# Four projections of a two-layer decoder trunk as seven half-products instead of eight, on one Trainium2 core

## The chip, the cores and the metric

The kernel runs on one core of a Trainium2 chip. TensorE (PE) multiplies matrices into PSUM, VectorE (DVE), ScalarE (ACT) and GpSimd (POOL) work on tiles, and the queue of SyncE (SP) issues the loads. The metric is device time in microseconds. The kernel before takes 1397.26 us, the median of 3 runs from 1395.95 to 1399.61.

## The reference

Input x is 512 tokens by 1024 features, c one conditioning vector. Two layers follow each other, then a final RMSNorm. Everything is fp32. One layer, cut to what matters:

```
h = rmsnorm(x, norm_w) * (1 + scale) + shift          # scale, shift, gate: from c @ w_ada
qa, ka, va, za, qr, kr, vr, zr, ga, gr = split(h @ w_in)   # 1536 x3, 512, 1024 x6 columns
y_att = dilated_attention(qa, ka, va) * silu(za)      # 512 x 512, three window patterns, joined by softmax
y_ret = groupnorm(retention(rot(qr), rot(kr), vr)) * silu(zr)   # 512 x 1024, four heads of 256
merged = sigmoid(ga) * (y_att @ w_proj_attn) + sigmoid(gr) * (y_ret @ w_proj_ret)
x = x + gate * (merged @ w_out)
```

The change concerns the products for ga, gr, y_ret @ w_proj_ret and merged @ w_out. Each is 512 x 1024 by 1024 x 1024.

## The kernel before

Every fp32 factor is split into a high part (a rounded copy) and a low part (the rest): `split` (L151) lets ScalarE cast the source to `hi` and VectorE subtract `hi` from the source to get `lo`. A product is then three matmuls, hi by hi, hi by lo and lo by hi (`mm3`, L175), accumulated in PSUM. Weights come from DRAM in tiles `wst` of 512 KB (128 partitions x 2 x 512 or 4 x 256 elements), issued on SyncE's queue (`weights`, L162), and are split into `wh` and `wl`.

The core does one thing after another for a layer: projections and attention for two pairs of head slots, then four retention heads (`ret_q`, `ret_k`, `ret_z`, `ret_scores`, `ret_v`, `ret_out`, `ret_y`), then gates, merge and output (`layer`, L754). Up to the merge the activations are feature-major: features on partitions, 512 tokens along a row, with the weights as the stationary side. `gate` (L700) makes 256 features of a gate at a time; `merge` (L708) multiplies the attention projection (4 blocks of 128 inputs) and the retention projection (8 blocks) by their gates and splits the sum; its result is the stationary side of `out_block` (L741), which makes one block of 128 tokens by 512 columns, token-major, from w_out held in SBUF (`out_weights`, L729). Blocks 0 to 3 of the second half of the columns end one after the other, and each that is complete calls `on_block`: at the end of layer 0 `next_layer` (L829), which normalizes the block and turns it for layer 1, at the end of layer 1 `result` (L843), which scales and stores it. x lives in four SBUF tiles `xb`, updated in place.

A tile scheduler orders each engine's instructions ahead of time, after the program's order and its own model of when what is ready. Tiles come from pools of a fixed count of slots for each tag (`NB`, L70); a tile whose slot is still in use waits. Work for the conditioning vector (`ada`, L197: a vector-matrix product on VectorE) and the gate rows is a `background` list, of which `step` (L157) does a piece at each weight load. All loads go through one queue, in the order in which they are issued.

## Time and profile before

| | us | share of the span |
|---|---|---|
| profiled execution | 1397.1 | |
| its span | 1395.3 | |
| TensorE busy | 1354.1 | 97% |
| VectorE busy | 833.5 | 60% |
| ScalarE busy | 487.7 | 35% |
| GpSimd busy | 161.3 | 12% |

TensorE is busy nearly from end to end; its granted clock over the span is 0.994 of full. The DMA engines move 106 GB/s on average, 148.06 MB in all. A row of the profile gives line, engine, operation, output and inputs; the time of one is its mean, and the idle time named with it is that of the engine just before it, with what ended it.

### The profile page before, as it was taken

The numbers are of one execution on the slowest core, as the hardware profiler recorded it, in microseconds if no ns is written. First come the engines' busy times: TensorE is split into PE (matmuls) and PEld (weight loads), VectorE is DVE, ScalarE is ACT, GpSimd is POOL, SyncE is SP. The second block draws the span as 40 slices with busy tenths as digits, with TensorE's granted clock in tenths as the row PEclk, the third lists the DMA queues.
The fourth block names the chain that finished last, engine by engine and source line by source line (L and its number), as shares of the span: only waits on it lengthen the run. The fifth ranks groups of instructions, "written<-read, shape, count | busy, mean of one in ns | idle before, by whom it ended". The sixth has DMA issues, their size and how long they took to land.

```text
span 1395.3 us, 17913 instructions
## 1 busy us (share of the span) xinstructions
PE 1354.1 (97%) x7033; PEld 1177.4 (84%) x7033; DVE 833.5 (60%) x1492; ACT 487.7 (35%) x863; POOL 161.3 (12%) x140
## 2 busy tenths in 40 slices
PE   3899999999999999999999999999999999999997
PEld 3778978888888888888888898888898898888886
DVE  6887678786547554335656646556745656533444
ACT  4352433253233243224333325234432233422322
POOL 3500000031102121000030001002111211100001
PEclk9899999999999999999999999999999999999999
DMA  9746145322222232224613232122232222222511
GB/s 309 229 151 181 61 137 166 112 71 84 79 96 91 69 98 91 91 91 159 201 49 106 76 91 90 61 91 76 76 92 75 91 89 71 91 91 91 169 42 61
DMA packets 136404, 148.06 MB, mean 106 GB/s; under 512 B 5056, under 2 KB 125056, under 8 KB 136320
## 3 DMA queue, kind: packets, MB, share of 16 engines
q1 hardware_dynamic: 136320, 146.92, 33.3%
q8 instruction: 55, 0.90, 0.3%
q14 instruction: 29, 0.24, 0.0%
HBM read 144.81 MB, written 2.10 MB: 105 GB/s over the span
## 4 chain that ended last, share of the span: by engine, by line
PE 90%; DVE 5%; DMA 1%; SPq 1%; issue 1%; ACT 1%; POOL 0%; POOLq 0%; DVEq 0%; ACTq 0%
PE ps_mm L180 80%; PE ps_aux L180 5%; PE ps_po L186 1%; DVE f L536 1%; SPq L194 1%; DVE acc L208 1%; PE ps_aux L565 1%; DVE wl L153 1%; PE ps_aux L186 1%; DMA pt<-in_w_ada 1%; PE ps_po L187 1%; PE ps_aux L679 1%; DMA v<-in_w_ada 0%; POOL h L294 0%; DVE qk L153 0%
## 5 line engine op out<-in xcount | busy, mean ns | idle before, releaser
L180 PE MATMUL ps_mm<-h,wh 128*128 128x512 f32 x2176 | 681.0, 393 | 5.1 <-DVE qk L153 2.1
L180 PEld LDWEIGHTS ps_mm<-h,wh 128*128 128x128 f32 x2176 | 406.7, 189 | 87.4 <-DVE qk L153 2.3
L180 PE MATMUL ps_mm<-h,wl 128*128 128x512 f32 x1088 | 424.6, 393 | 3.9 <-DVE wl L153 3.6
L153 DVE TENSOR_TENSOR wl<-wst,wh 128x1024 fp32r<-128x1024 f32 x194 | 244.7, 1264 | 227.7 <-ACT wh L152 225.4
L152 ACT CAST wh<-wst 128x1024 fp32r<-128x1024 f32 (+1 forms) x202 | 210.3, 1045 | 349.4 <-PE ps_mm L180 275.6
L180 PEld LDWEIGHTS ps_mm<-h,wl 128*128 128x128 f32 x1088 | 204.9, 189 | 46.1 <-DVE wl L153 4.5
L180 PE MATMUL ps_mm<-wh,h 128*128 128x256 f32 (+1 forms) x960 | 213.5, 316 | 0.2 <-POOL h L294 0.2
L180 PEld LDWEIGHTS ps_mm<-wh,h 128*128 128x128 f32 x960 | 180.8, 223 | 1.4 <-POOL h L294 0.6
L180 PE MATMUL ps_mm<-wl,h 128*128 128x256 f32 (+1 forms) x480 | 150.4, 315 | 0.0
L180 PEld LDWEIGHTS ps_mm<-wl,h 128*128 128x128 f32 x480 | 106.9, 223 | 0.2
L618 POOL TENSOR_TENSOR tmp<-tmp,tmp 128x512 f32<-128x512 f32 x32 | 49.2, 1554 | 458.6 <-ACT wh L152 234.1
L153 DVE TENSOR_TENSOR v<-ps_mm,v 128x256 fp32r<-128x256 f32 (+1 forms) x52 | 24.0, 463 | 61.7 <-ACT v L152 61.6
L152 ACT CAST qk<-ps_mm 128x512 fp32r<-128x512 f32 x48 | 27.8, 586 | 94.0 <-PE ps_mm L180 94.0
L208 DVE SCALAR_TENSOR_TENSOR acc<-pt,sc,acc 128x256 f32<-128x256 f32 x112 | 58.9, 526 | 2.6
L180 PE MATMUL ps_mm<-v,wh 128*128 128x512 f32 x192 | 59.1, 389 | 0.0
L152 ACT CAST v<-ps_mm 128x256 fp32r<-128x256 f32 (+1 forms) x52 | 20.9, 406 | 97.4 <-PE ps_mm L180 97.4
L180 PE MATMUL ps_aux<-qk,qk 128*128 128x256 f32 (+3 forms) x288 | 47.8, 307 | 0.0
L180 PEld LDWEIGHTS ps_aux<-qk,qk 128*128 128x128 f32 x288 | 42.9, 190 | 3.4
L153 DVE TENSOR_TENSOR qk<-ps_mm,qk 128x512 fp32r<-128x512 f32 x48 | 32.8, 686 | 19.6 <-ACT qk L152 19.6
L180 PEld LDWEIGHTS ps_mm<-v,wh 128*128 128x128 f32 x192 | 36.0, 188 | 7.5
L704 ACT ACTIVATE y<-ps_mm 128x512 f32<-128x512 f32 x32 | 19.0, 594 | 58.8 <-PE ps_mm L180 58.8
L180 PE MATMUL ps_mm<-s,wh 128*128 128x512 f32 x128 | 39.4, 389 | 0.0
(196 smaller groups left out, 1569.1 us busy)
## 6 DMA issues: line engine op xcount, KB each, us to landing
wst<-in_w_in SPq DMA_DIRECT2D x170, 512.0 KB, 3.6
pt<-in_w_ada SPq DMA_DIRECT2D x36, 512.0 KB, 5.0
wst<-in_w_proj_ret SPq DMA_DIRECT2D x16, 512.0 KB, 3.4
wst<-in_w_out SPq DMA_DIRECT2D x16, 512.0 KB, 3.6
qk<-in_w_ada SPq DMA_DIRECT2D x8, 512.0 KB, 8.6
wst<-in_w_proj_attn SPq DMA_DIRECT2D x8, 512.0 KB, 3.4
wst<-in_w_in SPq DMA_DIRECT2D x8, 384.0 KB, 6.6
v<-in_w_ada SPq DMA_DIRECT2D x8, 256.0 KB, 5.2
```

The lines of the kernel that those rows point to most:

```text
L152: nc.scalar.copy(hi, src)
L153: (nc.gpsimd if pool else nc.vector).tensor_tensor(lo, src, f(hi), op=ALU.subtract)
L180: nc.tensor.matmul(ps_ap, a, b_, start=first and i == 0, stop=last and i == n - 1, skip_group_check=skip)
L186: nc.tensor.matmul(ps_ap, st[0], mv, start=first, stop=False, skip_group_check=skip)
L187: nc.tensor.matmul(ps_ap[:, 0:P], st[1], mv[:, 0], start=False, stop=last, skip_group_check=skip)
L194: nc.sync.dma_start(s_, src[:, i:i + per])
L208: nc.vector.scalar_tensor_tensor(acc, w_, c_, acc, op0=ALU.mult, op1=ALU.add)
L536: nc.vector.tensor_copy(f0[32 * cc:32 * cc + 32, b], f0c[32 * b:32 * b + 32, cc])
L565: nc.tensor.transpose(blk(ps, j), src, ident)
L618: nc.gpsimd.tensor_tensor(a, a, b_, op=ALU.subtract if i == 0 else ALU.add)
L679: nc.tensor.transpose(ps[:, (2 * i + j) * P:(2 * i + j + 1) * P], self.rn[2 * b2 + j][:, i * P:(i + 1) * P], ident)
L704: nc.scalar.activation(s_, ps, AF.Sigmoid)
```

## The change

Each of the four products is cut in half along tokens, inner dimension and columns, into 2 x 2 blocks: A11 to A22 for the activations (256 tokens by 512 inputs), W11 to W22 for the weights (512 x 512). Eight products of blocks would be the plain way. `pair` does seven, with sums of blocks on either side: with S1 = A21 - A22, S2 = S1 - A11, S4 = S2 + A12 and S3 = A11 - A21, the products are A11 by W11, A12 by W21, S1 by (W11 + W12), S4 by W22, S2 by (W11 + W12 + W22), S3 by (W22 + W12) and A22 by (W11 + W12 + W22 + W21). They are done in the order 11, 12, S1, S4, S2, S3, 22, each as 24 matmuls of 512 columns with a token block as the stationary side, so the results are token-major. Outputs come from sums of products: block (0,0) after product 12, (0,1) after S2, (1,1) after S3, (1,0) after 22.

The weight sums are made while loading: `add` is a DMA on GpSimd's queue that adds the source in DRAM to a tile already in SBUF. One pair of tiles ("x") holds W11 and takes W12, W22 and W21 in turn, each after the split of the sum before; another ("z") holds W22 and takes W12; W21 is loaded plainly. The activation sums are made by `combined`: on GpSimd for h (used for both gates), on VectorE for retention's output (`combine_y`) and for the merged inputs (`combine_m`). `merge_att` makes the attention projection token-major, merges, and turns the merged blocks by TensorE. The multiplications by za move to the end of the last retention head. x is not kept in SBUF: it is loaded again at the output projection (`result`), from `x1d`, a DRAM tensor written by `next_layer`, in layer 1. The pools change: h, s, v and y have half as many slots of twice the size, and wst seven slots instead of three.

The core of the diff:

```
-    NB = dict(h=16, qk=6, s=8, v=12, pt=4, y=12, tmp=4, wst=3, wh=4, wl=4, dec=1)
+    NB = dict(h=8, qk=6, s=4, v=6, pt=4, y=6, tmp=4, wst=7, wh=4, wl=4, dec=1)
...
-    xb = [big.tile([P, D], F32, tag=f"x{b}", name=f"x{b}", bufs=1) for b in range(4)]
+    xs = [T("s", F32, (P, D)) for b in range(4)]
+    dram = ctx.enter_context(tc.tile_pool(name="dram", bufs=1, space=bass.MemoryType.DRAM))
+    x1d = dram.tile([S, D], F32, name="x1d")
...
+        def pair(self, src, rows0, nk, j0, A, buf, done):
+            step()
+            n = nk // 2
+            def part(r, c, i):
+                r0, c0 = rows0 + (r * n + 2 * i) * P, j0 + c * S
+                return src[r0:r0 + 2 * P, c0:c0 + S].rearrange("(k p) j -> p k j", p=P)
+            def load(r, c):
+                ts = [T("wst", F32, (P, 2, S)) for _ in range(n // 2)]
+                for i, t in enumerate(ts):
+                    nc.sync.dma_start(t, part(r, c, i))
+                return ts
+            def add(ts, r, c):
+                for i, t in enumerate(ts):
+                    nc.gpsimd.dma_start(t, part(r, c, i), accum_op=ALU.add)
+                return ts
+            def parts(ts):
+                res = []
+                for t in ts:
+                    hi, lo = T2("wh"), T2("wl")
+                    split(t, hi, lo)
+                    res.append((hi, lo))
+                return res
+            chain = {}
+            def weights_of(i):
+                if i == 0:
+                    chain["x"] = load(0, 0)
+                    return parts(chain["x"])
+                if i == 1:
+                    return parts(load(1, 0))
+                if i == 3:
+                    chain["z"] = load(1, 1)
+                    return parts(chain["z"])
+                return parts(add(chain["z"], 0, 1) if i == 5 else
+                             add(chain["x"], *{2: (0, 1), 4: (1, 1), 6: (1, 0)}[i]))
+            def product(a, w, ps, first):
+                for u in range(2):
+                    mm3(ps[u], [(A[a](k, u), (w[k // 2][0][:, k % 2], w[k // 2][1][:, k % 2])) for k in range(n)],
+                        first=first, skip=True)
+            b, c, e = [PS(), PS()], None, None
+            x1, x5 = {}, {}
+            names = ["11", "12", "S1", "S4", "S2", "S3", "22"]
+            ws = [weights_of(0)]
+            for i, a in enumerate(names):
+                if i + 1 < len(names):
+                    ws.append(weights_of(i + 1))
+                w = ws[i]
+                if i == 0:
+                    product(a, w, b, True)
+                    for u in range(2):
+                        x1[u] = buf(0, 0, u)
+                        nc.scalar.copy(x1[u], b[u])
+                elif i == 1:
+                    e = [PS("po"), PS("po")]
+                    product(a, w, e, True)
+                    for u in range(2):
+                        nc.vector.tensor_tensor(x1[u], e[u], x1[u], op=ALU.add)
+                        done(0, 0, u, x1[u])
+                elif i == 2:
+                    c = [PS(), PS()]
+                    product(a, w, c, True)
+                    for u in range(2):
+                        x5[u] = buf(1, 1, u)
+                        nc.scalar.copy(x5[u], c[u])
+                elif i == 3:
+                    product(a, w, c, False)
+                elif i == 4:
+                    product(a, w, b, False)
+                    for u in range(2):
+                        t = buf(0, 1, u)
+                        nc.scalar.copy(t, b[u])
+                        nc.vector.tensor_tensor(t, c[u], t, op=ALU.subtract)
+                        done(0, 1, u, t)
+                elif i == 5:
+                    product(a, w, b, False)
+                    for u in range(2):
+                        nc.vector.tensor_tensor(x5[u], x5[u], b[u], op=ALU.subtract)
+                        done(1, 1, u, x5[u])
                 else:
+                    product(a, w, b, False)
+                    for u in range(2):
+                        done(1, 0, u, b[u])
+        def combined(self, terms, n, tags, eng, own=True):
...
+            for name in ("S1", "S4", "S2", "S3"):
+                tile_(name)
+            for i in range(n // 2):
+                t = T("tmp").rearrange("p (k t) -> p k t", k=2)
+                a11, a12, a21, a22 = (terms(r, c, i) for r in range(2) for c in range(2))
+                def less(o, a, b):
+                    eng.tensor_tensor(o, a[0], b[0], op=ALU.subtract)
+                    if len(a) == 2:
+                        t2 = T("tmp").rearrange("p (k t) -> p k t", k=2)
+                        eng.tensor_tensor(t2, a[1], b[1], op=ALU.subtract)
+                        eng.tensor_tensor(o, o, t2, op=ALU.add)
+                less(t, a21, a22)
+                put("S1", i, t)
+                for a in a11:
+                    eng.tensor_tensor(t, t, a, op=ALU.subtract)
+                put("S2", i, t)
+                for a in a12:
+                    eng.tensor_tensor(t, t, a, op=ALU.add)
+                put("S4", i, t)
+                t3 = T("tmp").rearrange("p (k t) -> p k t", k=2)
+                less(t3, a11, a21)
+                put("S3", i, t3)
...
+        def gates(self, off, tag):
+            g = [T(tag, F32, (P, 2, S)) for _ in range(4)]
+            at = lambda r, c, u: g[2 * r + u][:, c]
+            self.pair(self.win, 0, KT, off, self.A, at,
+                      lambda r, c, u, ap: nc.scalar.activation(at(r, c, u), ap, AF.Sigmoid))
+            return g
+        def combine_y(self):
...
+            self.A = self.combined(terms, 4, ["s", "s", "v", "v", "h", "h", "h", "h", "qk", "qk", "qk", "qk", "qk", "qk"],
+                                   nc.vector)
+        def merge_ret(self):
+            def done(r, c, u, ap):
+                g = self.gr[2 * r + u][:, c]
+                nc.vector.tensor_tensor(g, ap, g, op=ALU.mult)
+            self.pair(w_proj_ret[self.l], 0, KT, 0, self.A, lambda r, c, u: T("tmp"), done)
+        def merge_att(self):
...
+            self.mT = [[T("y", F32, (P, 4, CW)) for c in range(2)] for r in range(2)]
+            for b in range(4):
+                for c in range(2):
+                    ps, g = PS(), self.ga[b][:, c]
+                    mm3(ps, [((blk(ya[k][0], b), blk(ya[k][1], b)), tuple(t[:, k % 2] for t in wa[2 * c + k // 2]))
+                             for k in range(4)])
+                    nc.vector.tensor_tensor(g, ps, g, op=ALU.mult)
+                    nc.vector.tensor_tensor(g, g, self.gr[b][:, c], op=ALU.add)
+                    ps = PS("aux")
+                    for k in range(4):
+                        nc.tensor.transpose(blk(ps, k), blk(g, k), ident)
+                    o = self.mT[b // 2][c][:, :, (b % 2) * P:(b % 2 + 1) * P]
+                    nc.scalar.copy(o, ps.rearrange("p (k t) -> p k t", k=4))
+        def combine_m(self):
...
+            self.A = self.combined(terms, 4, ["h"] * 8 + ["qk"] * 6, nc.vector)
+        def result(self, xin, on_block):
+            xt = []
+            for b in range(4):
+                xt.append(T("pt", F32, (P, D)))
+                nc.sync.dma_start(xt[b], xin[b * P:(b + 1) * P])
+            ssq = [small([P, 2], "ssq", 4) for b in range(4)]
+            left = [2] * 4
+            def done(r, c, u, ap):
+                b = 2 * r + u
+                cols = slice(c * S, (c + 1) * S)
+                t = T("tmp")
+                nc.vector.tensor_tensor(t, ap, gate_bc[self.l][:, cols], op=ALU.mult)
+                nc.vector.tensor_tensor(xt[b][:, cols], xt[b][:, cols], t, op=ALU.add)
+                nc.scalar.activation(t, xt[b][:, cols], AF.Square, accum_out=ssq[b][:, c:c + 1])
+                left[b] -= 1
+                if not left[b]:
+                    on_block(b, xt[b], rms(b, ssq[b]))
+            self.pair(w_out[self.l], 0, KT, 0, self.A, lambda r, c, u: T("tmp"), done)
...
-        L.ys, L.mg = [], []
-        L.split_y(0, 4)
-        ga = [L.gate(GA, 0)]
+        L.combine_h()
+        L.za(0)
         L.ret_out(RETH - 1)
-        gr = [L.gate(GR, 0)]
+        L.za(1)
+        L.ga = L.gates(GA, "v")
         L.ret_y(RETH - 1)
-        L.split_y(4, 12)
-        for m in range(1, 4):
-            ga.append(L.gate(GA, m))
-            gr.append(L.gate(GR, m))
-            L.merge(m - 1, ga[m - 1], gr[m - 1])
-        w0 = L.out_weights(0, ["h"] * 16)
-        L.merge(3, ga[3], gr[3])
-        ssq = [small([P, 3], "ssq", 4) for b in range(4)]
-        w1 = L.out_weights(1, ["v"] * 12 + ["s"] * 4)
-        for b in range(4):
-            L.out_block(0, b, w0, ssq)
-        for b in range(4):
-            L.out_block(1, b, w1, ssq)
-            on_block(b, rms(b, ssq[b][:, 0:3 if b == 3 else 2]))
+        L.gr = L.gates(GR, "pt")
+        L.combine_y()
+        L.merge_ret()
+        L.merge_att()
+        L.combine_m()
+        L.result(xin, on_block)
...
-    def next_layer(b, r):
-        xn.append(normalize(b, r))
+    def next_layer(b, x_, r):
+        nc.sync.dma_start(x1d[b * P:(b + 1) * P], x_)
+        xn.append(normalize(x_, r))
...
-    layer(L0, next_layer)
+    layer(L0, x, next_layer)
...
-    layer(L1[0], result)
+    layer(L1[0], x1d, result)
```

Three places show what moves. The first is VectorE at the output projection of layer 0. Before, it has there the gate and residual operations of the blocks (L750, L751; x_69 to x_72 are the four blocks of x) and the background's modulation (L208):

```order
L750 TENSOR_TENSOR tmp_5827<-ps_mm_5826,gate_89 128x512
L208 SCALAR_TENSOR_TENSOR acc_6248<-pt_6255,sc,acc_6248 128x256
L751 TENSOR_TENSOR x_69<-x_69,tmp_5827 128x512
L208 SCALAR_TENSOR_TENSOR acc_6248<-pt_6255,sc,acc_6248 128x256
L750 TENSOR_TENSOR tmp_5856<-ps_mm_5855,gate_89 128x512
L208 SCALAR_TENSOR_TENSOR acc_6248<-pt_6255,sc,acc_6248 128x256
L751 TENSOR_TENSOR x_70<-x_70,tmp_5856 128x512
```

After, from the last sums for S1 to the first operands of S4, between the products S1 and S2. Here y_5659 to y_5662 are the merged inputs, tmp_5851 and tmp_5865 the running sums (L838, L841 are `combined`), qk_5848, qk_5850, qk_5880 and h_5846 the low parts for S2, S3, 22 and S4, ps_po the sums of product 12 (L776), and wl_6042 the low part of the first weight tile for S2:

```order
L838 TENSOR_TENSOR tmp_5851<-tmp_5851,y_5659 128x512
L838 TENSOR_TENSOR tmp_5865<-tmp_5865,y_5659 128x512
L155 TENSOR_TENSOR qk_5848<-tmp_5851,qk_5847 128x512
L155 TENSOR_TENSOR qk_5848<-tmp_5865,qk_5847 128x512
L841 TENSOR_TENSOR tmp_5851<-tmp_5851,y_5660 128x512
L155 TENSOR_TENSOR qk_5850<-tmp_5861,qk_5849 128x512
L841 TENSOR_TENSOR tmp_5865<-tmp_5865,y_5660 128x512
L155 TENSOR_TENSOR qk_5850<-tmp_5875,qk_5849 128x512
L155 TENSOR_TENSOR qk_5880<-y_5662,qk_5879 128x512 x2
L155 TENSOR_TENSOR h_5846<-tmp_5851,h_5845 128x512
L776 TENSOR_TENSOR tmp_5947<-ps_po_5961,tmp_5947 128x512
L155 TENSOR_TENSOR wl_6042<-wst_5899,wh_6041 128x1024
```

The sums and splits of the merged inputs now stand on VectorE ahead of wl_6042.

The second place is VectorE at the boundary from layer 0 to layer 1. Before, at the end of the last token block (x_72; L293 modulates a turned block of layer 1, L282 normalizes, L146 is part of the root mean square):

```order
L750 TENSOR_TENSOR tmp_6102<-ps_mm_6101,gate_89 128x256
L750 TENSOR_TENSOR tmp_6131<-ps_mm_6130,gate_89 128x256
L751 TENSOR_TENSOR x_72<-x_72,tmp_6102 128x256
L751 TENSOR_TENSOR x_72<-x_72,tmp_6131 128x256
L293 TENSOR_SCALAR tmp_6174<-ps_aux_6169,mod_a_86,mod_s_88 128x256
L273 TENSOR_REDUCE ssum_6159<-ssq_5785 128x1
L146 TENSOR_SCALAR rn_t_6161<-ssum_6159 128x1
L293 TENSOR_SCALAR tmp_6178<-ps_aux_6169,mod_a_86,mod_s_88 128x256
L282 TENSOR_SCALAR y_6165<-x_72,rn_6163 128x512
L282 TENSOR_SCALAR y_6166<-x_72,rn_6163 128x512
```

After, from the first half of product 22 on (ps_mm_5897; pt_5889, pt_5891 and pt_5887 are blocks 2, 3 and 1 of x, L936 and L937 the gate and the residual addition, L285 normalizes, L296 modulates, L208 and L210 are the background, wl_6512 and wl_6518 weights of layer 1):

```order
L936 TENSOR_TENSOR tmp_6209<-ps_mm_5897,gate_92 128x512
L937 TENSOR_TENSOR pt_5891<-pt_5891,tmp_6181 128x512
L285 TENSOR_SCALAR y_6138<-pt_5887,rn_6135 128x512 x2
L208 TENSOR_SCALAR acc_6350<-pt_6351,sc 128x256
L937 TENSOR_TENSOR pt_5889<-pt_5889,tmp_6209 128x512
L155 TENSOR_TENSOR wl_6512<-wst_6509,wh_6511 128x1024
L210 SCALAR_TENSOR_TENSOR acc_6350<-pt_6351,sc,acc_6350 128x256
L155 TENSOR_TENSOR wl_6518<-wst_6515,wh_6517 128x1024
L296 TENSOR_SCALAR tmp_6236<-ps_aux_6231,mod_a_89,mod_s_91 128x256
L275 TENSOR_REDUCE ssum_6213<-ssq_5895 128x1
L210 SCALAR_TENSOR_TENSOR acc_6350<-pt_6351,sc,acc_6350 128x256
L148 TENSOR_SCALAR rn_t_6215<-ssum_6213 128x1
```

The residual additions of blocks 2 and 3 (L937) and weight subtractions (L155) now stand ahead of the first modulated block of layer 1 (L296).

The third place is GpSimd's queue from the last retention head to the retention projection of layer 0. Before, it has additions of rotated inputs (L618), splits of the mixers' results (L153) and small powers (L148):

```order
L618 TENSOR_TENSOR tmp_4394<-tmp_4394,tmp_4395 128x512
L618 TENSOR_TENSOR tmp_4402<-tmp_4402,tmp_4403 128x512
L153 TENSOR_TENSOR s_4893<-y_3462,s_4892 128x512
L153 TENSOR_TENSOR s_4901<-y_3936,s_4900 128x512
L153 TENSOR_TENSOR v_4669<-y_1680,v_4668 128x512
L153 TENSOR_TENSOR v_4677<-y_2669,v_4676 128x512
L153 TENSOR_TENSOR v_4909<-y_4410,v_4908 128x512
L148 TENSOR_TENSOR rs_4770<-rs_t_4768,mhalf 128x2
L148 TENSOR_TENSOR rs_4806<-rs_t_4804,mhalf 128x2
L153 TENSOR_TENSOR pt_4916<-y_4876,pt_4916 128x512
```

After, at the gates GA and GR: adding DMAs into staged weight tiles (wst_4740 and wst_4741 are the x pair of GA, wst_4830 and wst_4831 its z pair, wst_5029 and wst_5030 the x pair of GR):

```order
L624 TENSOR_TENSOR y_2639<-y_2639,tmp_4726 128x512
L624 TENSOR_TENSOR y_2639<-y_2639,tmp_4730 128x512
L729 DMA wst_4740<-in_w_in 128x2x512
L729 DMA wst_4741<-in_w_in 128x2x512
L729 DMA wst_4830<-in_w_in 128x2x512
L729 DMA wst_4831<-in_w_in 128x2x512
L729 DMA wst_4740<-in_w_in 128x2x512
L729 DMA wst_4741<-in_w_in 128x2x512
L729 DMA wst_5029<-in_w_in 128x2x512
L729 DMA wst_5030<-in_w_in 128x2x512
L729 DMA wst_5029<-in_w_in 128x2x512
L729 DMA wst_5030<-in_w_in 128x2x512
```

The splits are gone from GpSimd, and the adds stand there one behind the other, each waiting for the split of the tile that it adds to.

## Rows read from the trace of the kernel before

**Rows 1.** The page: busy time, chain by engine, two costly groups.

```profile
PE 1354.1 (97%) x7033; PEld 1177.4 (84%) x7033; DVE 833.5 (60%) x1492; ACT 487.7 (35%) x863; POOL 161.3 (12%) x140
...
PE 90%; DVE 5%; DMA 1%; SPq 1%; issue 1%; ACT 1%; POOL 0%; POOLq 0%; DVEq 0%; ACTq 0%
...
L153 DVE TENSOR_TENSOR wl<-wst,wh 128x1024 fp32r<-128x1024 f32 x194 | 244.7, 1264 | 227.7 <-ACT wh L152 225.4
...
L208 DVE SCALAR_TENSOR_TENSOR acc<-pt,sc,acc 128x256 f32<-128x256 f32 x112 | 58.9, 526 | 2.6
```

**Rows 2.** Windows: us, busy time by engine (instructions), granted clock, DMA share, GB/s.

```profile
37.00:48.00 11.00, 8.67 (x31) 6.98 (x30) 10.17 (x22) 3.51 (x5) 6.97 (x3) 0.62 1.09 350
536.00:716.00 180.00, 180.00 (x826) 150.22 (x825) 89.11 (x128) 57.68 (x85) 5.12 (x7) 1.00 0.36 117
716.00:743.00 27.00, 26.80 (x177) 24.15 (x176) 19.18 (x38) 12.68 (x26) 10.79 (x15) 1.00 0.31 98
1208.00:1388.00 180.00, 180.00 (x822) 150.14 (x820) 79.32 (x101) 54.17 (x82) 8.12 (x8) 1.00 0.27 89
```

**Rows 3.** Chain, pieces in order of time: start us, us, what.

```profile
435.10 0.87 PE ps_aux L679 x8
...
487.61 0.87 PE ps_aux L679 x8
...
1213.78 168.67 PE ps_mm L180 x744
```

**Rows 4.** ScalarE's groups from 1210 to 1390 us, by form.

```profile
L152 ACT CAST wh<-wst 128x1024 fp32r<-128x1024 f32 x22 | 23.2, 1054 | 37.5 <-PE ps_mm L180 33.3 <-DMA wst<-in_w_proj_ret 2.5 <-DMA wst<-in_w_proj_attn 1.6
...
L152 ACT CAST qk<-y 128x512 fp32r<-128x512 f32 x6 | 3.7, 624 | 18.8 <-DVE y L722 18.8
```

**Rows 5.** VectorE's groups of the same stretch.

```profile
L153 DVE TENSOR_TENSOR wl<-wst,wh 128x1024 fp32r<-128x1024 f32 x22 | 26.9, 1225 | 48.4 <-ACT wh L152 48.4
...
L715 DVE TENSOR_TENSOR y<-ps_mm,y 128x512 f32<-128x512 f32 x8 | 5.5, 690 | 5.5 <-PE ps_mm L180 5.3
...
L153 DVE TENSOR_TENSOR qk<-y,qk 128x512 fp32r<-128x512 f32 x6 | 4.1, 690 | 2.8 <-ACT qk L152 2.8
```

**Rows 6.** DMA: first of three queues; issues, KB each, median us to landing.

```profile
q1 hardware_dynamic: 136320, 146.92, 33.3%
...
wst<-in_w_in SPq DMA_DIRECT2D x170, 512.0 KB, 3.6
...
qk<-in_w_ada SPq DMA_DIRECT2D x8, 512.0 KB, 8.6
```

**Rows 7.** GpSimd's groups over the whole run, by form.

```profile
L618 POOL TENSOR_TENSOR tmp<-tmp,tmp 128x512 f32<-128x512 f32 x32 | 49.2, 1554 | 458.6 <-ACT wh L152 234.1 <-DVE tmp L617 114.8 <-issue 109.8
...
L294 POOL TENSOR_TENSOR h<-tmp,h 128x256 fp32r<-128x256 f32 x16 | 12.3, 780 | 10.5 <-DVE tmp L293 10.2
```

**Rows 8.** VectorE near the end, in time: start us, us, line, operation, idle before.

```profile
1374.94 1.77 DVE L852 SCALAR_TENSOR_TENSOR y<-x,rn,y 128x512 f32<-128x512 f32 x1 [0.66 <-POOL rn L148]
...
1382.47 0.69 DVE L750 TENSOR_TENSOR tmp<-ps_mm,gate 128x512 f32<-128x512 f32 x1 [0.39 <-PE ps_mm L180]
...
1388.22 0.42 DVE L750 TENSOR_TENSOR tmp<-ps_mm,gate 128x256 f32<-128x256 f32 x1 [0.32 <-PE ps_mm L180]
...
1390.74 0.75 DVE L852 SCALAR_TENSOR_TENSOR y<-x,rn,y 128x512 f32<-128x512 f32 x1 [0.66 <-POOL rn L148]
```

**Rows 9.** TensorE in the opening, in time.

```profile
43.65 0.79 PE L180 MATMUL ps_mm<-h,wh 128*128 128x512 f32 x1 [0.99 <-POOL h L294]
...
44.67 0.63 PE L180 MATMUL ps_mm<-h,wh 128*128 128x512 f32 x1
45.10 0.63 PE L180 MATMUL ps_mm<-h,wl 128*128 128x512 f32 x1
```

**Rows 10.** GpSimd near the end, in time.

```profile
1374.87 1.30 POOL L854 TENSOR_TENSOR y<-x,y 128x512 f32<-128x512 f32 x1
```

## The prediction

> **What bounds the kernel now.** I read the page first, by engine and by chain. TensorE is busy for 97% of the span and carries 90% of the chain that ended last; VectorE is busy for 60% [rows 1]. An average hides stages, so next I read the windows. The stretch that the change rewrites, from the gates to the end of the output projection, has TensorE busy for all of its 180 us in either layer, with VectorE at 79 to 89 us, ScalarE at 54 to 58 and DMA share at 0.27 to 0.36 [rows 2]. The chain there is one piece of 744 matmuls in 168.67 us [rows 3], so 0.2267 us for one of 512 columns. A matmul taken away there is worth its full price, as long as what feeds its successors still comes in time; a feeder has about half of the stretch left to grow into. The layer boundary is as tight: TensorE works 26.80 of 27 us [rows 2].

> **What is removed.** Eight half-products of 24 matmuls become seven, in four projections and two layers: 8 x 24 = 192 matmuls of 512 columns, 192 x 0.2267 = 43.5 us. All of it lies on the path.

> **What is added to TensorE.** The attention projection now gives token-major blocks, which have to be turned: 32 transposes of 128x128 per layer. Eight of the kind take 0.87 us [rows 3], so 64 x 0.109 = 7.0 us. The gross gain is 36.5 us, and the full gain from this execution's 1397.1 us is 1360.6. (That execution lies 0.2 us under the median of the runs shown.)

> **What the feeders get.** A product now has its own weight sum: 7 MB read per projection instead of 4, in 7 x 24 x 0.2267 = 38.1 us, a mean of 193 GB/s. Each of the 14 staged tiles costs a cast of 1.05 us on ScalarE [rows 4] and a subtraction of 1.23 us (1.26 over the whole run) on VectorE [rows 1, 5]: 14.8 and 17.6 us of 38.1. For the gates come six combinations of 0.69 us (4.1 us) on VectorE, which leaves it under 60%: I cost GA and GR at nothing, hidden behind their own matmuls. For retention's projection there are besides the splits and sums of its inputs, by my count some 35 us of VectorE in 38.1: full, but not over. Without that cover each further us counts.

> **The adding DMAs.** Four of a projection's seven weight sets are made by adding into a tile already staged; sets 11, S1, S2 and 22 use one pair of tiles in turn (the third listing's wst_4740 and wst_4741). An add may start only when the tile has been split (1.05 + 1.26 = 2.3 us) and its sum is wanted two products later, 10.9 us. So an add of up to 10.9 - 2.3 = 8.6 us from issue to landing costs nothing; beyond that three adds in the chain lag, against about 4.5 us of slack, since a set is made one product ahead. The kernel before has one hardware queue for its loads and no adding DMA [rows 6]. Bounds: a plain load of 512 KB lands after 3.6 us; the slowest of that size, in the crowded opening, after 8.6 [rows 6]. An add can hardly be quicker than the load. I take 7, about two loads' time, since an add has its target to read too: no term in the sum, and the whole of it in a rival. [...]

> **The output projection, where I put the loss.** In the first ordered listing of after, VectorE must finish the sums and splits of the merged inputs before TensorE can go on with S2: wl_6042, which the third matmul of S2 reads, stands behind them. From the last addition of the attention merge to it I count five weight subtractions (5 x 1.26 = 6.3 us) and 18 operations of 512 columns (18 x 0.69 = 12.4), 18.7 us. TensorE has for the same stretch four transposes (0.4), the last 8 matmuls of product 12, the 24 of S1 and two of S2: 34 x 0.2267 = 7.7, with 0.2 of start 8.3 us. It stands for 10.4 us per layer, say 11 with the copies of ScalarE between (0.62 each [rows 4]). Nothing hides it: the inputs of all four late products come from the same blocks. Two layers: +22 us. Below: 0, if the order is better spread than I read it, or the queue has less before it; above: 15 per layer, with the next weights late too.

> **The layer boundary.** Before, the four token blocks became complete one after the other, 5.4 us apart. Now blocks 2 and 3 both close only with product 22, the last. From the end of its first half VectorE has, by the second listing, two gate multiplications, two residual additions, two normalizations and a backlog of weight subtractions and modulation (0.53 each [rows 1]) up to the first modulated block: some 9.5 us, then an addition of 0.78 on GpSimd [rows 7]. TensorE has 2.7 us of the second half and 1.3 of transposes: it waits for about 6 us, then for 2 to 3 more while VectorE hands out the rest. I take +8.5, once; between 0 (as before) and 13.

> **Tail and the rest.** The last block's columns were cut in two so that little was left after the last matmul; now it has 512 columns: a multiplication and an addition of 0.69 instead of 0.42 [rows 8], and block 2's beside them: +1. x kept in DRAM adds 12 transfers of 512 KB, all asked for long before use: nothing. [...]

> **GpSimd beside VectorE.** The 20 sums of h per layer go to GpSimd, at 1.3 to 1.55 us each [rows 7, 10], 26 to 31 us during the end of retention. The trace shows what that does to the neighbour: the final scaling on VectorE takes 1.77 us beside a GpSimd operation of 1.30 and 0.75 alone [rows 8, 10]. [...] At worst 20 x 1.3 = 26 us of VectorE per layer; VectorE has idle time there, since it is busy for about half of each stage, so I take 0, and up to 8 in the range.

> **Sum.** -43.5 + 7.0 + 22 + 8.5 + 1 = -5.0, which is -5 us on 1397.1: 1392.

> **Rivals.**
> (B) The waits are hidden: VectorE's queue runs ahead or the stalls are some 3 us. For it: 80 us of VectorE in 180 before. Against: the order at the output projection. Time: 1360.6 + 1 + 2 x 3 = 1368, between 1358 and 1378.
> (C) The slower side: the adds are the bound, at one place, the chain of sets 11, S1, S2, 22. For it: an add's own time is in no row, it reads twice, and loads and adds together mean (7 + 4) MB in 38.1 us, 303 GB/s, what the crowded opening moved at a DMA share of 0.96 to 1.09 [rows 2]. Against: 3.6 us for a plain load at a share of 0.3. Each of 8 projections lags by 3 x (L - 8.6) - 4.5. At L = 10.3 that is 0.6, 5 us in all, and the gain is gone: from there it decides. L = 11 gives 2.7 x 8 = 22: 1414. L = 12 gives 5.7 x 8 = 46: 1438. L = 14 gives 94: 1486.
> [...]
> That the change saves no matmuls I dismiss: its list for TensorE is shorter, and each of the seven products stands there once.

> **How the numbers follow.** My forecast (A) has 0.42, B 0.18, C 0.22, D 0.18. A's own range is 1378 to 1402. About 0.3% (4.2 us) can be told from no change in this kernel, so faster means under 1393 and slower over 1401.5. A splits into 0.28 faster, 0.11 same, 0.03 slower; B is faster, C slower, D 0.03 same and 0.15 slower. Faster 0.46, same 0.14, slower 0.40. The range is 1364 to 1440: it leaves out B's best third (0.06) and C from L = 12 on (0.13).

> **What would show it.** TensorE's rows: 192 fewer matmuls of 512 columns at the same spacing, or the first step is wrong. In the output projection TensorE should stop twice, at the start of S1 and of S2, for a subtraction on VectorE, some 10 us per layer; if it doesn't stop, B. The adding DMAs' time from issue to landing decides C: under 8.6 us and no wait of a cast on a DMA in the middle of a projection, or over 10 and TensorE stopping once in each of the eight projections with a DMA as releaser. At 716 us of before, now some 18 us earlier, TensorE should pause for 8 us. [...] I am wrong in kind if TensorE stops inside the gate projections, or if retention's stage, which the change hardly touches, is longer than its 52.5 us per head (from 435.1 to 487.6 between two of its transposes [rows 3]).

## The result, and the profile after

The changed kernel takes 1541.51 us, the median of 4 runs (1539.92 to 1543.85), against 1396.61: 1.1035 times the time before, interval 1.1012 to 1.1057. The forecast was 1392 with a range from 1364 to 1440. The matmuls that were to go are gone: 144 of 512 columns and 96 of 256 fewer, the work of 192 of 512, and 64 transposes more, which is why the page below counts 176 instructions less than [rows 1]. TensorE is busy for 89% of a longer span.

The page of the changed kernel, with the lines that answer to [rows 1, 6]:

```profile
PE 1364.5 (89%) x6857; PEld 1167.3 (76%) x6857; DVE 967.7 (63%) x1648; ACT 583.0 (38%) x991; POOL 284.8 (18%) x232
...
q0 software_dynamic: 17408, 33.56, 13.6%
...
PE 57%; issue 21%; DVE 9%; POOL 6%; DMA 5%; ACT 1%; SPq 0%; POOLq 0%; ACTq 0%; DVEq 0%
...
wst<-in_w_in POOLq DMA_DIRECT2D x32, 512.0 KB, 5.9
```

An add lands after 5.9 us, well under the 8.6 that were to cost nothing, and yet "issue", time in which an engine waits for nothing that the profile shows, holds 21% of the chain. Where that is, GpSimd's rows in time show (start us, us, operation, idle before):

```profile
546.60 1.21 POOL L729 DMA_DIRECT2D wst<-in_w_in  x1 [6.11 <-issue]
552.89 1.21 POOL L729 DMA_DIRECT2D wst<-in_w_in  x1 [5.08 <-DVE tmp L829]
558.92 1.20 POOL L729 DMA_DIRECT2D wst<-in_w_in  x1 [4.82 <-issue]
564.96 1.21 POOL L729 DMA_DIRECT2D wst<-in_w_in  x1 [4.84 <-issue]
```

The adds start 6.0 to 6.3 us apart. The last two add to different tiles (the x pair, for product 22) and hold no wait for each other; the second still starts 6.04 us after the first. ScalarE's and then TensorE's rows show what hangs on it:

```profile
558.70 1.04 ACT L154 CAST wh<-wst 128x1024 fp32r<-128x1024 f32 x1 [4.99 <-DMA wst<-in_w_in]
559.65 0.58 ACT L790 COPY v<-ps_mm 128x512 f32<-128x512 f32 x1
```

```profile
560.28 0.80 PE L182 MATMUL ps_mm<-wh,qk 128*128 128x512 f32 x1 [7.87 <-ACT v L790]
...
624.01 0.80 PE L182 MATMUL ps_mm<-wh,qk 128*128 128x512 f32 x1 [13.81 <-ACT pt L790]
```

The add issued at 552.89 has landed at 558.70, and 0.22 us later, at 558.92, the next one starts: one at a time. The cast waits for its add, behind it in ScalarE's order stands the copy of the finished S2, and TensorE, which finished S2 at 552.4, waits for that copy. The windows of that stretch, in the columns of [rows 2]:

```profile
540.00:580.00 40.00, 26.25 (x90) 19.61 (x89) 17.29 (x22) 12.51 (x18) 6.53 (x6) 0.83 0.59 121
580.00:620.00 40.00, 28.58 (x125) 22.93 (x123) 20.43 (x23) 18.15 (x24) 7.30 (x6) 0.94 0.63 120
...
660.00:700.00 40.00, 24.10 (x83) 17.73 (x82) 15.57 (x18) 10.20 (x11) 4.87 (x4) 0.79 0.55 131
```

In these three windows TensorE is busy for 24 to 29 us of 40 (36 in the one between them), at a mean granted clock of 0.79 to 0.94; the transfer engines are busy for 0.55 to 0.63. So eight adds of 6.05 us, 48.4 us of queue per projection, set the pace where 38.1 us of matmuls should.

### The profile page after: what moved, and what is told of

The parts are those of the page before. It is cut to its first block, busy times and chain, and to the rows that moved or that the text cites. A ratio compares the mean times of both kernels' runs of the same rounds, so it can differ in the third digit from the quotient of the medians.

```text
span 1540.2 us, 18134 instructions
## 1 busy us (share of the span) xinstructions
PE 1364.5 (89%) x6857; PEld 1167.3 (76%) x6857; DVE 967.7 (63%) x1648; ACT 583.0 (38%) x991; POOL 284.8 (18%) x232
## 3 DMA queue, kind: packets, MB, share of 16 engines
q0 software_dynamic: 17408, 33.56, 13.6%
## 4 chain that ended last, share of the span: by engine, by line
PE 57%; issue 21%; DVE 9%; POOL 6%; DMA 5%; ACT 1%; SPq 0%; POOLq 0%; ACTq 0%; DVEq 0%
PE ps_mm L182 48%; PE ps_aux L182 4%; POOL wst L729 3%; DVE wl L155 2%; DMA wst<-in_w_out 2%; PE ps_po L188 1%; DVE f L551 1%; DMA wst<-in_w_proj_ret 1%; PE ps_po L182 1%; POOL tmp L838 1%; DVE qk L155 1%; ACT wh L154 1%; PE ps_aux L580 1%; DVE tmp L210 1%; PE ps_aux L188 1%
## 5 line engine op out<-in xcount | busy, mean ns | idle before, releaser
L182 PE MATMUL ps_mm<-h,wh 128*128 128x512 f32 x1664 | 523.4, 393 | 6.0 <-POOL h L297 3.6
L155 DVE TENSOR_TENSOR wl<-wst,wh 128x1024 fp32r<-128x1024 f32 x258 | 334.6, 1301 | 302.1 <-ACT wh L154 299.7
L154 ACT CAST wh<-wst 128x1024 fp32r<-128x1024 f32 (+1 forms) x266 | 275.1, 1043 | 496.9 <-PE ps_mm L182 247.6
L182 PEld LDWEIGHTS ps_mm<-h,wh 128*128 128x128 f32 x1664 | 310.0, 189 | 68.8 <-POOL h L297 4.4
L182 PE MATMUL ps_mm<-wh,h 128*128 128x256 f32 (+1 forms) x1248 | 317.7, 342 | 23.2 <-ACT h L154 9.1
L182 PE MATMUL ps_mm<-h,wl 128*128 128x512 f32 x832 | 325.6, 392 | 3.6 <-DVE wl L155 3.6
L182 PE MATMUL ps_mm<-wh,qk 128*128 128x512 f32 x384 | 142.8, 442 | 98.2 <-ACT pt L790 27.5
L182 PEld LDWEIGHTS ps_mm<-wh,qk 128*128 128x128 f32 x384 | 82.5, 215 | 126.6 <-ACT pt L790 28.4
L182 PE MATMUL ps_mm<-wl,qk 128*128 128x512 f32 x192 | 83.9, 439 | 3.4 <-DVE wl L155 3.4
L182 PE MATMUL ps_mm<-wh,s 128*128 128x512 f32 x224 | 72.2, 392 | 0.0
L155 DVE TENSOR_TENSOR v<-ps_mm,v 128x256 fp32r<-128x256 f32 (+1 forms) x52 | 24.0, 463 | 54.5 <-ACT v L154 54.5
L210 DVE SCALAR_TENSOR_TENSOR acc<-pt,sc,acc 128x256 f32<-128x256 f32 x112 | 56.6, 505 | 2.1
```

Of the source, the lines that this page charges most:

```text
L154: nc.scalar.copy(hi, src)
L155: (nc.gpsimd if pool else nc.vector).tensor_tensor(lo, src, f(hi), op=ALU.subtract)
L182: nc.tensor.matmul(ps_ap, a, b_, start=first and i == 0, stop=last and i == n - 1, skip_group_check=skip)
L210: nc.vector.scalar_tensor_tensor(acc, w_, c_, acc, op0=ALU.mult, op1=ALU.add)
```

## The experiments

Four questions stood: is it the addition, GpSimd's queue, or the rest of the change? If the queue, what in it? What are the other terms worth? And is there a version that keeps the gain?

**Plain copies on the same queue.**

```
-                    nc.gpsimd.dma_start(t, part(r, c, i), accum_op=ALU.add)
+                    nc.gpsimd.dma_start(t, part(r, c, i))
```

> The adding DMAs become plain copies on the same queue of GpSimd, into the same tiles (the weight sums are left out). In the changed kernel adds that wait for nothing else start 6.05 us apart. Theory Q: the software queue itself lets one transfer of 512 KB go in 6 us, whatever it does; then copies are 6 us apart too, and the time stays near 1541. Rival A: the addition is slow, since it reads two sources; then copies are 3 to 4 us apart and the time falls to 1390 to 1430. Rival R: the transfers are not the loss, the rest of the change is; then the spacing may change and the time stays over 1480.

1395.8 us, from one run. The copies do not wait for each other:

```profile
531.19 0.77 POOL L729 DMA_DIRECT2D wst<-in_w_in  x1 [2.16 <-DVE wl L155]
532.45 0.73 POOL L729 DMA_DIRECT2D wst<-in_w_in  x1 [0.49 <-DVE wl L155]
```

Theory Q in its form "6 us whatever the transfer does" falls; R falls too, and the time is the one that rival A gave. But a copy is also described with fewer packets, 9216 for the 64 of them (144 each) against 272 for an add:

```profile
q0 software_dynamic: 9216, 33.56, 7.8%
```

**Plain loads on SyncE's queue.**

```
-                    nc.gpsimd.dma_start(t, part(r, c, i), accum_op=ALU.add)
+                    nc.sync.dma_start(t, part(r, c, i))
```

> The adding DMAs become plain loads on SyncE's hardware queue, into the same tiles at the same places of the program (the weight sums are left out, so is the software queue). Theories Q and A: what is left of the change is the sum of the prediction, about 1392, or 1368 if its waits at the output projection are hidden. Rival R: over 1480.

1392.05 us, 0.9965 of before (0.9952 to 0.9979): the sum of the prediction to the microsecond, though not term by term (below). All of the 149.5 us that the forecast missed come from how the sums are made.

**Each add in two halves.**

```
-                    nc.gpsimd.dma_start(t, part(r, c, i), accum_op=ALU.add)
+                    for j in range(2):
+                        nc.gpsimd.dma_start(t[:, j], part(r, c, i)[:, j], accum_op=ALU.add)
```

> Each adding DMA of 512 KB is cut into two of 256 KB. If a fixed time of a DMA sets the 6.05 us, the adds stay about 6 us apart, there are twice as many, 97 us per projection instead of 48, and the time goes to about 1900. If bytes or descriptors set it, they are 3 us apart and the time stays near 1541.

1447.66 us, from one run: neither. Twice as many adds of the same bytes gave back 94 us. GpSimd's rows:

```profile
533.49 2.71 POOL L730 DMA_DIRECT2D wst<-in_w_in  x3 [1.44 <-DVE wl L155]
538.08 0.88 POOL L730 DMA_DIRECT2D wst<-in_w_in  x1 [1.88 <-issue]
540.06 0.87 POOL L730 DMA_DIRECT2D wst<-in_w_in  x1 [1.11 <-DVE wl L155]
```

```profile
q0 software_dynamic: 18432, 33.56, 14.9%
```

Three halves go at once, then a fourth waits. In packets: three of 144 (432) fit, two of 272 (544) don't. My guess from these counts is a store that is full; the next runs put it to the test. A number that could be its size stands in the program that builds the kernel, before and after: `dynamic_dma_scratch_size=1024`; the page of the kernel before has no software queue at all.

**A larger store,** paid for with one staged slot, its control, and a middle size:

```
-    NB = dict(..., tmp=4, wst=7, ...)
+    NB = dict(..., tmp=4, wst=6, ...)
...
-    nc = bacc.Bacc(..., dynamic_dma_scratch_size=1024)
+    nc = bacc.Bacc(..., dynamic_dma_scratch_size=4096)   # e10: 2048; the control: 1024
```

> The changed kernel with a larger scratch area for the descriptors of GpSimd's DMA queue (4096 bytes of each partition instead of 1024), paid for by one staged weight slot (6 instead of 7). Theory K: the adds are one at a time because the queue's descriptors fill that area: an add of 512 KB is 272 packets (17408 over 64) and goes alone, of the halves with 144 packets each (18432 over 128) three go together and a fourth waits, so the room is between 432 and 544 packets. With four times the room seven adds fit; they start as soon as their tile is split, and the time falls to 1400 to 1430, near the copies' 1396. Rival A: the addition itself keeps the transfer engines busy for 6 us; then the spacing stays 6 us and the time at 1530 to 1550.

> The control for the run before: the changed kernel with 6 staged weight slots and the scratch area as it was. Theory K and rival A alike: the adds stay 6 us apart and the time within 10 us of 1541.

> As e5, with the descriptor area at 2048 bytes: by theory K room for 864 to 1088 packets, three full adds at once. A projection has at most four adds asked for at about the same time, so nearly all of the gain of e5 should come: 1399 to 1415. By a limit of another kind (only one add at a time unless the area is over some size) it stays at 1539.

1399.07 us with 4096 (e5; ratio to before 1.0013, 1.0002 to 1.0024), 1538.81 for the control, 1397.55 with 2048, just under the range given; the last two are one run each. In the control the adds are still 6 us apart:

```profile
561.62 1.20 POOL L729 DMA_DIRECT2D wst<-in_w_in  x1 [4.89 <-issue]
567.59 1.21 POOL L729 DMA_DIRECT2D wst<-in_w_in  x1 [4.76 <-issue]
```

With 4096, GpSimd's queue:

```profile
532.54 2.45 POOL L729 DMA_DIRECT2D wst<-in_w_in  x2 [2.16 <-DVE wl L155]
537.14 1.20 POOL L729 DMA_DIRECT2D wst<-in_w_in  x1 [2.15 <-DVE wl L155]
538.88 1.19 POOL L729 DMA_DIRECT2D wst<-in_w_in  x1 [0.54 <-DVE wl L155]
...
575.32 1.20 POOL L729 DMA_DIRECT2D wst<-in_w_in  x1 [0.53 <-DVE wl L155]
```

No "issue" is left before an add: of the 53 idle stretches before an add 49 end when a tile is split (two adds follow in 2.45 us), four when a transfer lands. The add at 575.32 is the fourth in a row. With 2048 the same one starts a little later, and the profile names a landing as what released it, as theory K's room for three would have it:

```profile
575.96 1.20 POOL L729 DMA_DIRECT2D wst<-in_w_in  x1 [1.35 <-DMA wst<-in_w_in]
```

One number of the build, with the same instructions for the adds, is worth 140 us; theory K stands as far as these runs go, and A falls for good. That the number is a room which descriptors fill is my reading of its name and of the packet counts; the runs show what follows when it is changed, not what it holds. Beside plain loads (1392.05) the adds now cost 7 us, with one staged slot less.

**Sums by GpSimd, and by VectorE.**

```
-                    nc.gpsimd.dma_start(t, part(r, c, i), accum_op=ALU.add)
+                    raw = T("wst", F32, (P, 2, S))
+                    nc.sync.dma_start(raw, part(r, c, i))
+                    nc.gpsimd.tensor_tensor(t, t, raw, op=ALU.add)      # e7: nc.vector
```

> The weight sums are made by GpSimd instead of by adding DMAs: the block is loaded plainly on SyncE's queue into a tile of its own, and one addition of 1024 columns adds it, 2.6 to 3.1 us by twice the 512-column rows (1.30 to 1.55), 21 to 25 us per projection of 38.1. Theories Q and A: 1392 to 1420, the upper end if VectorE is slowed beside GpSimd. Rival R: over 1480.

> The weight sums by VectorE: plain loads on SyncE's queue into tiles of their own and one addition of 1024 columns each, 8 x 1.26 = 10 us more of VectorE per projection. By the sums of VectorE's work GA and GR stay under their 38.1 us (32), retention's projection goes to 45 and the output projection to 59 against 49 before: 7 + 10 us per layer, 1392 + 34 = 1426 (1415 to 1440). Rival: VectorE's adds are hidden by its idle time, then 1395 to 1405.

By GpSimd 1459.51 us (1.0446, 1.0425 to 1.0467), 40 us over my upper end. GpSimd's additions took the time foreseen; what suffered is the neighbour. First GpSimd's group, then VectorE's, in that run:

```profile
L731 POOL TENSOR_TENSOR wst<-wst,wst 128x1024 f32<-128x1024 f32 x64 | 186.7, 2930 | 204.7 <-DVE wl L155 197.0 <-DMA wst<-in_w_proj_ret 7.7
```

```profile
L155 DVE TENSOR_TENSOR wl<-wst,wh 128x1024 fp32r<-128x1024 f32 x258 | 382.9, 1495 | 119.1 <-ACT wh L154 117.0 <-PE ps_mm L182 1.3
```

The weight subtraction takes 1495 ns on average; with plain loads the same 258 took 329.6 us:

```profile
L155 DVE TENSOR_TENSOR wl<-wst,wh 128x1024 fp32r<-128x1024 f32 x258 | 329.6, 1283 | 153.9 <-ACT wh L154 149.6 <-PE ps_mm L182 2.6
```

That is 53 us more of VectorE in all, the collision of [rows 8, 10]; it was weighed for the sums of h and not for this. TensorE's waits for `wl` rose with it, from 5.3 to 29.4 us; the rest of the 67 us over the plain loads was not taken apart. By VectorE, with the same tiles, 1413.53 us (1.0114, 1.0096 to 1.0133), just under the range given: retention's projection was hidden against my count (TensorE 60.00 of 60 us at 600 to 660), the output projection not, with VectorE busy for 66.50 of 70 us:

```profile
660.00:730.00 70.00, 56.83 (x250) 45.71 (x248) 66.50 (x98) 40.21 (x64) 6.97 (x7) 0.90 0.62 203
```

**Half-products for the gates alone, feature-major.** `product` multiplies with the roles exchanged, the merge is feature-major again and the output projection plain, as before (but x comes from DRAM, and the first half of the columns is summed for all four token blocks together), the sums are made by VectorE. The core of the edit:

```
-                    mm3(ps[u], [(A[a](k, u), (w[k // 2][0][:, k % 2], w[k // 2][1][:, k % 2])) for k in range(n)],
-                        first=first, skip=True)
+                    for t in range(2):
+                        cols = slice((2 * u + t) * P, (2 * u + t + 1) * P)
+                        mm3(ps[u][:, t], [((w[k // 2][0][:, k % 2, cols], w[k // 2][1][:, k % 2, cols]), A[a](k))
+                                          for k in range(n)], first=first and t == 0, skip=True)
```

> Half-products only for the two gates, and feature-major (weight sums stationary, 256 tokens moving), so no transposes; weight sums by VectorE as in the run before; retention's, attention's and output projection as in the kernel before. 4 x 24 matmuls fewer, 21.8 us: 1375 if VectorE's 32 us stay under the 38.1 of a gate, the layer boundary is as before and nothing else waits. If the splits that now come after the gates hold up the merge, or VectorE the gates, 1380 to 1392. Rival: halves don't pay here at all, since VectorE or the loads take back what is saved; then over 1395.

1390.06 us, 0.9946 (0.9925 to 0.9967): faster, but by 7.6 us where 21.8 were counted. The window at the gates, in the columns of [rows 2]:

```profile
570.00:610.00 40.00, 40.00 (x312) 38.91 (x311) 31.64 (x31) 24.34 (x31) 0.00 (x0) 1.00 0.65 201
```

TensorE is never idle, VectorE is where it was expected, and the weight-load side, busy for 38.91 of 40 us, is the likely limit. Matmuls of 256 columns follow each other at 0.12 us, not at half of 0.2267: a half-product of 48 takes 5.76 us instead of 5.44, so seven save 43.5 - 40.3 = 3.2 us per gate, 13 us for four. The other 5 us were not followed. The kernel before had already shown the price, where its last block is cut in two; 18 matmuls take 2.16 us there:

```profile
1385.15 2.32 PE L180 MATMUL ps_mm<-v,qk 128*128 128x256 f32 x18
1387.31 0.88 PE L180 MATMUL ps_mm<-s,pt 128*128 128x256 f32 x6
```

**Half-products for gates and retention, output projection plain,** with the store of 4096:

```
-        L.combine_m()
+        L.split_m()
...
-            self.pair(w_out[self.l], 0, KT, 0, self.A, lambda r, c, u: T("tmp"), done)
...
+            w = [p for kp in range(4) for p in self.out_load(0, kp, tags)]
+            for b in range(4):
+                ps = PS()
+                mm3(ps, [(mg(k, b), w[k]) for k in range(KT)])
+                close(b, 0, 0, 1, ps)
...
```

`split_m` makes the high and low parts of the merged inputs, without sums. The weights of one half of the columns are held in SBUF, and one token block of 24 matmuls follows the other; the second half of the columns is done likewise.

> The larger descriptor area (4096) and 6 staged slots as in e5, and half-products for the gates and retention's projection only; the output projection is plain, eight products, one token block after the other as in the kernel before (its weights held in SBUF), so combined inputs, late blocks and their stalls are gone. By the terms of the sum: 1360.6 (all four projections, nothing waits) + 48 matmuls given back, 10.9 us = 1371.5, and some us for the splits of the merged inputs: 1372 to 1382. If the loss of e5 (1399) lies not in the output projection and the layer boundary but in the adds' load on the transfers, it stays over 1390.

1383.24 us, 0.9897 (0.9881 to 0.9914): 14 us faster than before and the fastest of all, 1 us over the range given. Giving back 10.9 us of matmuls made the run 15.8 us shorter than the one with four: all that seven products bring with them at the output costs 26.7 us. The same window in the run with the store of 4096 alone, then in this one:

```profile
660.00:720.00 60.00, 49.10 (x209) 38.30 (x208) 51.27 (x80) 34.13 (x56) 13.27 (x13) 0.91 0.81 203
```

```profile
660.00:720.00 60.00, 57.79 (x314) 49.74 (x313) 46.14 (x79) 24.89 (x46) 9.27 (x13) 0.97 0.66 207
```

## Why the prediction was wrong

**Where it failed.** The step "an add of up to 10.9 - 2.3 = 8.6 us from issue to landing costs nothing" took the latency of one add for its whole price. It supposed that the adds of a product's two tiles, and of the x and z chains, run side by side. Latency was 5.9 us, below even the 7 taken; but only one add was under way at a time, so it became an occupation: 48.4 us per projection. The prediction's own sign of being wrong in kind came true: TensorE stopped inside the gate projections, 7.87 and 13.81 us in the rows above. Its test for C could not see why, since it looked at an add from its issue on, and the wait lies before the issue. Rival C, the adds as bound, had the right place and the wrong mechanism: it hung on L, with the gain gone at 10.3, and the median of L never came near: with the store of 4096, where adds do run side by side, it was 6.4 to 7.3 us by source. (Copies on the same queue landed after 4.1 to 4.8: source by source an add took 1.4 to 1.6 times as long.) What I had not asked of a queue that the trace of before doesn't use is how much it may hold. The code could have raised the question: a new kind of transfer beside a setting that the kernel before had no use for. The large store against the control is 1538.81 - 1399.07 = 139.7 us, 17.5 per projection; another 7 of the 149.5 are adds against loads on SyncE's queue (1399.07 - 1392.05), and 2.7 lie between the changed kernel and the control.

**What held.** The matmuls fell by 192, and eight of the new transposes take 0.79 us where 0.87 was counted (665.04 to 665.83 with the store of 4096); with the sums free of charge the time was 1392.05 for a sum of 1392. GA, GR and retention's projection ran nearly without stops where weights came in time, with the store of 4096:

```profile
530.00:600.00 70.00, 69.63 (x309) 57.01 (x308) 53.49 (x64) 46.07 (x64) 19.76 (x17) 1.00 0.86 191
600.00:660.00 60.00, 59.94 (x270) 49.38 (x269) 40.02 (x47) 26.00 (x32) 7.24 (x6) 1.00 0.72 178
```

The output projection stopped TensorE where I had put it, at S1 and S2; that run's rows:

```profile
676.09 0.50 PE L182 MATMUL ps_mm<-wh,h 128*128 128x512 f32 x1 [1.81 <-ACT h L154]
...
678.98 1.17 PE L182 MATMUL ps_mm<-wh,h 128*128 128x512 f32 x2 [1.68 <-DVE h L155]
679.95 0.63 PE L182 MATMUL ps_mm<-wl,h 128*128 128x512 f32 x1
680.38 1.05 PE L182 MATMUL ps_mm<-wh,h 128*128 128x512 f32 x2
681.23 0.63 PE L182 MATMUL ps_mm<-wl,h 128*128 128x512 f32 x1
...
686.47 0.50 PE L182 MATMUL ps_mm<-wh,qk 128*128 128x512 f32 x1 [0.50 <-ACT tmp L771]
...
688.11 0.50 PE L182 MATMUL ps_mm<-wl,qk 128*128 128x512 f32 x1 [1.14 <-DVE wl L155]
...
715.07 0.39 PE L182 MATMUL ps_mm<-wh,h 128*128 128x256 f32 x1 [1.54 <-ACT h L292]
...
719.17 0.80 PE L182 MATMUL ps_mm<-wh,h 128*128 128x256 f32 x2 [3.36 <-POOL h L297]
```

**Which sizes were off.** The stops at S1 and S2 are 5.1 us in layer 0 and 4.5 in layer 1, not 11 each. The operations were counted rightly, their times not. From the last transposes to the subtraction that S2 waits for, VectorE works for 15.6 us (672.42 to 688.06) where I had 18.7: its 18 operations of 512 columns start 0.60 apart and not 0.69, as the mean of one let me count, weight subtractions 1.14 apart and not 1.26, and one of the five comes before the transposes. TensorE's own work in that stretch takes 11.2 us, not 8.3; 1.7 of it is the clock, by estimate from the spacing: after the stops of 1.81 and 1.68 us eight matmuls take 3.5 us where 0.2267 each makes 1.8, at first 0.43 apart as in [rows 9], where the granted clock was 0.50 from 43 to 46 us. VectorE's spacing (same run):

```profile
682.03 0.69 DVE L841 TENSOR_TENSOR tmp<-tmp,y 128x512 f32<-128x512 f32 x1
682.63 0.69 DVE L155 TENSOR_TENSOR qk<-tmp,qk 128x512 fp32r<-128x512 f32 x1
683.23 0.69 DVE L841 TENSOR_TENSOR tmp<-tmp,y 128x512 f32<-128x512 f32 x1
```

The boundary's stops come to 6.3 us, the two longest 4.9, not 8.5; and they begin at 713.5 us, not some 18 us before 716, a reading that left out the 11 us of the sum's own output term. Against that stands the clock after such stops, which is not in the sum: 0.91 over the 60 us of that window, some 60 x 0.09 = 5.4 us of TensorE's work by estimate. Output and boundary together cost 26.7 us where I had 30.5, but the stops in that are only 16 us. The clock and waits not followed made up for the rest, so that the whole sum came out at 1392 to the microsecond is luck.

**Left open.** By estimate the queue's 48.4 us against 38.1 explain 10.3 us per projection, some 82 of the 140. The rest, such as the gaps between one projection's adds and the next one's and TensorE's lower clock (a mean of 0.952 against 0.987 with the store of 4096), was not taken apart. The 11.7 us by which the last version stays over 1371.5 are partly short stops at the boundary (1.81 us the longest); the rest was not followed.

## What to carry to other kernels

A transfer of a kind or on a queue that the kernel did not use has two prices, its latency (here 5.9 us) and how many may be under way (here one); one row of a neighbour (a plain load, 3.6 us) bounds the first and says nothing of the second. Where an engine waits and the profile calls it "issue", with the next start falling on the last landing (here 0.22 us after it), look for a limit on what may be under way. Cut the transfer in two: here that gave back 94 us and made such a limit likely, and a larger number in the build, worth 140 us, decided it. And of an algorithm that saves matmuls, apply it where its extra sums have time: three projections with it (1383.24 us) beat four (1399.07).
